# A key selection moved from a block of its own into the loops of two attentions

## The chip, the core and the metric

The kernel is one program on one core of a Trainium2 chip. The metric is the device time of one execution in microseconds (us). TensorE does the matrix products; VectorE, ScalarE and GpSimd work on vectors; SyncE issues the transfers from the chip's memory. The profile calls them PE, DVE, ACT, POOL and SP.

## The reference, cut to what matters

512 tokens of width 1024 go through a first block with four kinds of sequence mixers and a feed-forward part, and then through two layers of a second block. A layer of the second block is a feed-forward part, four mixers side by side, and another feed-forward part. The four mixers have four heads of 64 each: MLA (softmax attention on low-rank queries and keys), NSA (a compressed, a selected and a windowed softmax attention, weighted by gates), DSA (softmax attention on chosen keys) and stick-breaking attention. Their outputs are normalized in groups and multiplied by one output matrix. The part that matters here is DSA, which chooses for each query the 128 keys with the highest index scores:

```
n_top = min(DSA_TOPK, S // 4)                     # 128
rel = relu(einsum('bqhd,bsd->bqhs', qi, k_idx))
score = einsum('bqh,bqhs->bqs', wi, rel)
score = where(k_pos <= q_pos, score, NEG_INF)
_, idx = lax.top_k(score, n_top)
...                                               # softmax attention over the keys idx alone
```

## The kernel before

Queries and keys come in four tiles of 128 tokens. A query tile `i` sees the first `i + 1` key tiles, so the scores of tiles 1, 2 and 3 are 256, 384 and 512 columns wide; tile 0 needs no choice. The large products run as three passes over a high and a low part of each factor; ScalarE writes the high part of the weights and VectorE the low part (lines 447, 448, 454 and 455), and these pieces have high priority.

The code names only the engine of each instruction. A planner sets the order at compile time: it runs through the program in a simulated time, and on each engine takes, of the instructions whose inputs are ready there, the one that stands earliest in the program (or has high priority). On the chip each engine then works through its own list in that fixed order. `_dep` (line 335) adds an order between two instructions to what the planner has to keep; it is declared `NoSync`, so between two instructions of one engine it is their place in the list and nothing else.

`mixers` (line 1250) writes out one layer in this order:

- index queries and keys, then `dsa_score` (line 1451): the index scores of tiles 1 to 3, added up over eight heads on VectorE (line 1480) into `acc`;
- `compress`, then `stick` (line 1632) in turns with the projections of the other mixers, `mla_prep` (line 1383), and the compressed part of `nsa` (line 1569);
- `center` (line 576): the mean over the features is taken off the residual stream;
- the first attention (MLA, `attend` with `mla[0]`, line 1314), in turns with the stacking of NSA's queries and keys and with the product of the stick-breaking output (`out_part(3, ...)`);
- the second attention (NSA, line 1316), in turns with the product of the first one's output;
- `dsa_top` (line 1486): for each of the tiles 1 to 3, 16 rounds. A round finds the eight largest scores of each row (`max`, line 1496) and overwrites them in place (`match_replace`, line 1497; the profile shows a value load and a replacement for it). After 16 rounds the overwritten places are the 128 chosen keys, and line 1498 makes the mask `sel`;
- the third attention (DSA), whose scores take `sel` in through one more product, and the products that are left.

`attend` (line 1354) has eight units: two pairs of heads times four query tiles. A unit of MLA has two softmaxes (`softmax_t`, line 913), one of NSA four. A softmax is: scores on TensorE, the row maximum on VectorE (line 924), the exponential on ScalarE, a guard and the reciprocal on VectorE (lines 931 and 932), scaling on GpSimd (line 934 or 936), transposes on TensorE (line 939), a copy on ScalarE, and the product with the values. `interleave` (line 285) draws one unit from each generator in turn, and so sets the place in the program.

Of the kernel before, what the change touches and what calls it, by code (L numbers as in the profile page):

```python
# [14 lines left out]
ALU = mybir.AluOpType  # L15
# [18 lines left out]
# ---------------------------------------------------------------- host layout  # L34
# [3 lines left out]
def _blocks_t(w):  # L38
    """[K, C] -> chunks of at most RAW columns per partition: [128, blocks of 128 columns, K/128, 128], flat."""
    k, c = w.shape  # L40
    kt = k // 128
    t = w.reshape(kt, 128, c // 128, 128).transpose(1, 2, 0, 3)
    n, per = c // 128, RAW // k
    return np.concatenate([t[:, i:i + per].reshape(-1) for i in range(0, n, per)])


def _blocks_m(w):
    """[K, C] -> per 256 columns: [128, K/128, 256], flat."""
    k, c = w.shape
    return w.reshape(k // 128, 128, c // 256, 256).transpose(2, 1, 0, 3).reshape(-1)  # L50
# [24 lines left out]
def _small(w, axis):  # L75
    """The narrow columns of the first projection on rows 0, 32, 64 and 96 of one block."""
    def z(n):
        s = list(w.shape)
        s[axis] = n
        return np.zeros(s, w.dtype)  # L80

    def c(n):
        sl = [slice(None)] * w.ndim
        sl[axis] = _cols(IN1, n)
        return w[tuple(sl)]

    return np.concatenate([c("mi"), z(28), c("mf"), z(28), c("ga"), z(16), c("ff"), z(28)], axis=axis)


# rows of a head of 64 that is turned: the two of a pair lie 16 apart, as in a head of 32  # L90
# [183 lines left out]
# ---------------------------------------------------------------- device  # L274
def turns(*gens):
    """The units of several generators in turn."""
    gens = list(gens)
    while gens:
        for g in list(gens):
            try:  # L280
                next(g)
            except StopIteration:
                gens.remove(g)
            else:
                yield
# [11 lines left out]

class Builder:
# [17 lines left out]
    # -- small helpers  # L316
# [23 lines left out]
    def table(self, s):  # L340
        """Functions of one table set run together: what follows waits for what came before."""
        if s == self.set:
            return
        b = self.nc.scalar.preload_act_table_set(self.LOADS[s])  # L344
        for g in self.group:
            self._dep(b, g)
        if self.barrier is not None:
            self._dep(b, self.barrier)
        self.set, self.group, self.barrier = s, [], b
# [15 lines left out]
    def add_p(self, out, a, b, op=ALU.add):  # L365
        """out = a op b on GpSimd."""
        self.nc.gpsimd.tensor_tensor(out, a, b, op)
# [13 lines left out]
    def stack_q(self, tag, z, eng):  # L381
        """Two heads of 64 rows, each as its high and low parts one above the other; the high part where the head
        lay."""
        res = []
        for s, e in enumerate(eng):
            q = self.t(tag, dt=F32R)
            a, b = slice(64 * s, 64 * s + 64), slice(64 - 64 * s, 128 - 64 * s)
            self.copy_a(q[a], z[a])
            e.tensor_tensor(q[b], z[a], q[a].bitcast(F32), ALU.subtract)
            res.append(q)  # L390
        return res

    def stack_k(self, tag, z, a, eng):
        """64 rows a of z: their high part twice, their low part twice."""
        hi, lo = self.t(tag, dt=F32R), self.t(tag, dt=F32R)
        for s in range(2):
            self.copy_a(hi[64 * s:64 * s + 64], z[a])
        for s, e in enumerate(eng):
            e.tensor_tensor(lo[64 * s:64 * s + 64], z[a], hi[a].bitcast(F32), ALU.subtract)
        return hi, lo  # L400

    def stacked(self, ps, q, k, h, i):
        """Scores of head h of query tile i, K = 64, at full rate (256 columns at least)."""
        w = max(256, (i + 1) * 128)
        cs, r = slice(i * 128, i * 128 + 128), slice(64 * (h % 2), 64 * (h % 2) + 64)
        self.mm(ps[:, :w], q[h][:, cs], k[0][:, :w], True, False)
        self.mm(ps[:, :w], q[h][r, cs], k[1][r, :w], False, False)

    # -- weights
    def wstream(self, name, nhalf, F, lo_pool=False, center=False, tag=None, alt=()):  # L410
        """Blocks of the weights, F columns each: a list of pieces (hi, lo). center: the mean over all columns is
        taken off each row (for all blocks in one chunk). The pieces lie in tiles of `tag` if it is given; so do the
        blocks in `alt`, in tiles of "PT"."""
# [47 lines left out]
    @staticmethod  # L461
    def cut(pieces, c=128):
        """(hi, lo) of c columns each."""
        return [(hi[:, o:o + c], lo[:, o:o + c]) for hi, lo in pieces for o in range(0, hi.shape[1], c)]
# [9 lines left out]
    def lead(self, jobs, xs):  # L474
        """Up to four blocks (weights, epilogue) side by side, one half of the tokens after the other."""
        ps = [self.p(tag) for tag in ("mm", "mm", "T", "T")[:len(jobs)]]
        for cs in HALVES:
            for k in range(len(xs)):
                for o, (w, _) in zip(ps, jobs):
                    self.passes(o, w, k, xs[k], cs, len(xs))  # L480
        for o, (_, epi) in zip(ps, jobs):
            epi(o)
# [4 lines left out]
    def gemm_blocks(self, name, nblk, xs, epi, lead=0, lo_pool=False, center=False, hold=0, st=None):  # L487
        """out[block of 128 columns, token] for each block; xs: (hi, lo) per 128 rows of the weights.
        The first `lead` blocks run side by side, one half of the tokens after the other. The last `hold` blocks
        follow the attention."""  # L490
# [15 lines left out]
    def gemm_halves(self, name, xs, epi, between, center):  # L506
        """As gemm_t for few rows of weights, all of them on chip: first the one half of the tokens."""
# [14 lines left out]
    def gemm_m_blocks(self, name, ncol, xs, epi, lo_pool=False):  # L522
        """out[token, 256 columns]; epi(chunk, token tile, psum)."""
# [15 lines left out]
    # -- norms  # L539
    def rstd(self, out, in_, scale, eps):  # L540
        """(scale * in + eps) ** -0.5"""
# [3 lines left out]
    def rms_full(self, xs, gain):  # L545
        """rms_norm over all features of the blocks xs; (hi, lo) per block."""
# [23 lines left out]
    def center(self, xs, after=None):  # L570
        """The mean over all features is taken off xs."""
# [16 lines left out]
    class Norm:  # L588
        """x * gain / sqrt(mean(x ** 2) + eps) (+ beta) over blocks of features that are completed one by one,
        first for one half of the tokens. In place or apart."""  # L590
# [7 lines left out]
        def add(self, d, cs):  # L598
            """Squares, added up in pairs."""
# [37 lines left out]
    # -- everything  # L637
# [29 lines left out]
    # ================================================================ first block  # L667
# [147 lines left out]
    def log_sigmoid(self, out, x, tmp):  # L815
        """min(x, 0) - log(1 + exp(-|x|))"""
# [11 lines left out]
    def row(self, r, sign=1):  # L828
        """lhsT that spreads row r over 128 partitions (with all 128 rows as the contraction)."""
# [5 lines left out]
    def keep(self, ap, pattern_sign, base, op):  # L835
        """Zero where not (pattern_sign * (free - partition) + base op 0)."""
# [76 lines left out]
    def softmax_t(self, i, scores, gate=None, add=None):  # L913
        """P^T of query tile i of a causal softmax: [keys, key tile, queries]. scores fills a psum tile;
        add: something to add to the scores."""
# [16 lines left out]
        nc.vector.reciprocal(st[:, 2:3], st[:, 1:2])  # L932
# [208 lines left out]
    # ================================================================ second block  # L1141
    def ffn(self, f, l, xs, hl, norm):
        """alpha x + 0.5 swiglu(x), in place; returns the norm of that."""
# [95 lines left out]
    def rope(self, x, *parts):  # L1239
        """In place. parts: (dimension of the heads, their rows)."""  # L1240
# [9 lines left out]
    def mixers(self, l, hl, xs, norm, last):  # L1250
# [63 lines left out]
        interleave(self.attend(l, mla[0], y, 0), chain([None] * 2, nsa[1]()),  # L1314
                   out_part(3, True, normed(3)))
        interleave(self.attend(l, nsa[0], y, 1), out_part(0, False, normed(0)))
        res1 = normed(1)
        sel = self.dsa_top(accs)
# [35 lines left out]
    def attend(self, l, srcs, y, n, cuts=(slice(0, S),)):  # L1354
        """Four heads of 64. srcs(h, i): list of ("att", scores, gate, value of key tile j) or
        ("mm", lhsT, rhs) for query tile i, whose results add up."""
# [94 lines left out]
    def dsa_score(self, l, iq, misc, tok, accs):  # L1451
        """The products of high and low parts lie one above the other: high, low, high of a query's head on high,
        high, low of the key."""
# [32 lines left out]
    def dsa_top(self, accs):  # L1486
        """Per query tile, 0 for chosen keys and a large negative number for the others."""
        nc = self.nc
        tile = self.t("sel", (128, 1280), BF16)
        sel = [tile[:, 0:128], tile[:, 128:384], tile[:, 384:768], tile[:, 768:1280]]  # L1490
        nc.vector.tensor_copy(sel[0], self.negT)
        for i in range(1, NT):
            acc = accs[i]
            m8 = self.t("m8", (128, 8))
            for r in range(16):
                nc.vector.max(m8, acc)
                nc.vector.match_replace(acc, m8, acc, -3e38)
            nc.vector.tensor_scalar(sel[i], acc, -2e38, NEG, ALU.is_ge, ALU.mult)
        return sel
# [15 lines left out]
    def compress(self, l, cmp):  # L1515
        """Compressed keys (twice, one above the other) and values (four times)."""
# [29 lines left out]
        # gelu(x) = x / (1 + exp(-2 c (x + 0.044715 x^3)))  # L1546
# [22 lines left out]
    def nsa(self, l, comp, nq, nk, tok, res):  # L1569
        nc = self.nc  # L1570
        kc, vc = comp
        # gates
# [124 lines left out]
```

## Time and profile before

| what | value |
|---|---|
| time, median of 3 runs | 3370.67 us (3363.62 to 3381.74) |
| profiled execution, span | 3371.6 us |
| TensorE busy | 3267.3 us (97%) |
| VectorE busy | 1664.1 us (49%) |
| ScalarE busy | 1248.5 us (37%) |
| GpSimd busy | 425.8 us (13%) |
| mean granted clock of TensorE | 0.973 of 2.4 GHz |

The rows further down come from one profiled execution. "Busy" is the time in which an engine works on an instruction; a TensorE that is busy needn't be at its peak. The granted clock is the share of full speed at which TensorE was let run: 1.00 is 2.4 GHz, 0.50 is 1.2 GHz. "Idle before" is an engine's idle time ahead of an instruction, with the one that ended it. Times of day are us from the start of the span. The first layer's mixers lie from about 1410 to 1850 us, the second layer's some 1158 us later.

### The profile page before, as it was taken

The page shows a single profiled execution, that of the slowest core. Times are in us where ns is not written, and L with a number is a line of the kernel's source. Part 1 is how long each engine was busy: PE and PEld are TensorE (multiplying, and loading weights), DVE is VectorE, ACT ScalarE, POOL GpSimd, SP SyncE. Part 2 cuts the span into 40 slices and gives each one's busy share as a digit, 9 for nine tenths or more (in the row PEclk, how much of TensorE's full clock was granted, in tenths as well). Part 3 has the DMA queues.
Part 4 walks back from the last instruction along what each step waited for, and adds up shares of the span by engine and source line. Part 5 has one row for each costly group of instructions (what it writes and reads, how often), then busy time and mean ns, then how long its engine had stood idle before and what let it go on. Part 6 is the DMA issues. An engine that isn't in the chain of part 4 may idle for free.

```text
span 3371.6 us, 41243 instructions
## 1 busy us (share of the span) xinstructions
PE 3267.3 (97%) x16394; PEld 2642.9 (78%) x16398; DVE 1664.1 (49%) x2801; ACT 1248.5 (37%) x2225; POOL 425.8 (13%) x509
## 2 busy tenths in 40 slices
PE   8999999999999999999899999999999998999998
PEld 7798787888888888886567888788888764688887
DVE  4245444454333333579845333553336886453335
ACT  4354624343222222345544322332223445542223
POOL 0001001100000000231523000120004223220002
PEclk9999999999999999999879999999999897899999
DMA  3222222322222222321000222222222310012222
GB/s 134 85 75 79 78 97 85 118 88 100 97 91 100 88 96 92 113 89 53 26 26 26 100 100 89 99 76 100 88 100 76 103 45 31 14 51 100 100 91 72
DMA packets 53071, 275.58 MB, mean 82 GB/s; under 512 B 11136, under 2 KB 16144, under 8 KB 22416
## 3 DMA queue, kind: packets, MB, share of 16 engines
q1 hardware_dynamic: 52736, 272.83, 23.0%
q8 instruction: 129, 2.11, 0.3%
q14 instruction: 62, 0.51, 0.0%
q10 hardware_dynamic: 144, 0.12, 0.0%
HBM read 267.69 MB, written 2.10 MB: 80 GB/s over the span
## 4 chain that ended last, share of the span: by engine, by line
PE 87%; DVE 7%; ACT 3%; issue 1%; POOL 1%; DMA 1%; SPq 0%; ACTq 0%; DVEq 0%; POOLq 0%
PE mm L370 72%; PE S L370 6%; PE T L370 4%; PE O L370 4%; PE T L939 2%; POOL x L630 1%; DVE x L586 1%; DVE wlo L455 1%; DMA wraw<-ffn_w 1%; DVE yc L1245 1%; DVE x L620 0%; ACT L344 0%; ACT whi L363 0%; DVE gt L448 0%; DVE acc L1480 0%
## 5 line engine op out<-in xcount | busy, mean ns | idle before, releaser
L370 PE MATMUL mm<-ahl,whi 128*128 128x512 f32 (+1 forms) x5104 | 1552.1, 384 | 19.2 <-DVE ahl L634 7.6
L370 PEld LDWEIGHTS mm<-ahl,whi 128*128 128x128 f32 x5104 | 944.6, 189 | 216.5 <-issue 11.4
L363 ACT ACTIVATE whi<-wraw 128x1024 fp32r<-128x1024 f32 (+1 forms) x457 | 481.9, 1056 | 1500.7 <-PE mm L370 1406.1
L370 PE MATMUL mm<-ahl,wlo 128*128 128x512 f32 (+1 forms) x2552 | 971.9, 382 | 0.2
L455 DVE TENSOR_TENSOR wlo<-wraw,whi 128x1024 fp32r<-128x1024 f32 (+1 forms) x451 | 573.6, 1273 | 666.3 <-ACT whi L363 658.3
L370 PE MATMUL mm<-hz,whi 128*128 128x512 f32 x1792 | 560.2, 394 | 1.3 <-DVE x L1175 1.3
L370 PEld LDWEIGHTS mm<-ahl,wlo 128*128 128x128 f32 x2552 | 481.8, 189 | 94.8 <-DVE wlo L455 2.8
L370 PEld LDWEIGHTS mm<-hz,whi 128*128 128x128 f32 x1792 | 336.1, 188 | 81.2 <-DVE x L1175 3.0
L370 PE MATMUL mm<-hz,wlo 128*128 128x512 f32 x896 | 352.3, 394 | 0.0
L574 POOL TENSOR_TENSOR ss<-x,x 128x512 f32<-128x512 f32 x6 | 8.7, 1444 | 1564.5 <-DVE x L1175 1564.5
L370 PEld LDWEIGHTS mm<-hz,wlo 128*128 128x128 f32 x896 | 168.2, 188 | 39.8
L370 PE MATMUL mm<-whi,ahl 128*128 128x256 f32 x896 | 170.1, 289 | 7.2 <-DVE hz L1280 6.3
L1157 DVE SCALAR_TENSOR_TENSOR tA<-mm,tA 128x512 f32<-128x512 f32 x80 | 55.2, 690 | 242.3 <-PE mm L370 242.3
L370 PEld LDWEIGHTS mm<-whi,ahl 128*128 128x128 f32 x896 | 143.2, 194 | 11.8 <-DVE hz L1280 6.8
L370 PE MATMUL mm<-wlo,ahl 128*128 128x256 f32 x448 | 128.2, 287 | 1.5 <-DVE wlo L455 1.5
L1175 DVE TENSOR_TENSOR x<-x,mm 128x512 f32<-128x512 f32 x64 | 43.5, 685 | 140.4 <-PE mm L370 140.1
L924 DVE TENSOR_REDUCE sm<-S 128x1 f32<-128x256 f32 (+3 forms) x128 | 61.9, 487 | 97.9 <-PE S L370 91.0
L363 ACT ACTIVATE PT<-T 128x128 f32<-128x128 f32 (+3 forms) x146 | 63.4, 440 | 112.6 <-PE T L939 108.1
L370 PE MATMUL O<-PT,hz 128*64 128x128 f32 (+2 forms) x776 | 92.3, 299 | 2.2 <-ACT PT L363 2.2
L363 ACT ACTIVATE hz<-tA 128x512 fp32r<-128x512 f32 (+1 forms) x124 | 76.0, 617 | 48.3 <-DVE tA L800 40.6
L374 DVE TENSOR_TENSOR hz<-tA,hz 128x512 fp32r<-128x512 f32 (+1 forms) x124 | 82.4, 669 | 20.2 <-ACT hz L363 19.7
L370 PEld LDWEIGHTS mm<-wlo,ahl 128*128 128x128 f32 x448 | 86.9, 194 | 2.6 <-DVE wlo L455 2.1
(350 smaller groups left out, 3687.5 us busy)
## 6 DMA issues: line engine op xcount, KB each, us to landing
wraw<-ffn_w SPq DMA_DIRECT2D x132, 1024.0 KB, 4.8
wraw<-w_gate SPq DMA_DIRECT2D x16, 1024.0 KB, 4.8
wraw<-w_up SPq DMA_DIRECT2D x16, 1024.0 KB, 4.8
wraw<-w_dn SPq DMA_DIRECT2D x16, 1024.0 KB, 4.8
wraw<-w_br SPq DMA_DIRECT2D x8, 1024.0 KB, 4.8
wraw<-w_out SPq DMA_DIRECT2D x8, 1024.0 KB, 4.8
wraw<-w_o SPq DMA_DIRECT2D x4, 768.0 KB, 4.3
gt<-PT SPq DMA_DIRECT2D x48, 64.0 KB, 2.0
```

What stands on the lines that cost most here:

```text
L363: self.nc.scalar.activation(out, in_, AF.Copy)
L370: return self.nc.tensor.matmul(out, lhsT, rhs, start=start, stop=stop, skip_group_check=True)
L374: self.nc.vector.tensor_tensor(lo, src, hi.bitcast(F32), ALU.subtract)
L455: nc.vector.tensor_tensor(lo, r, hi.bitcast(F32), ALU.subtract)
L574: i = nc.gpsimd.tensor_tensor(s1, xs[0], xs[1], ALU.add)
L586: nc.vector.tensor_tensor(xs[d], xs[d], m0, ALU.subtract)
L630: nc.gpsimd.tensor_scalar(y, y, 1.0, be, ALU.mult, ALU.add)
L924: nc.vector.reduce_max(st[:, 0:1], ps, axis=AX.X, negate=True)
L939: nc.tensor.transpose(pt[:, j * 128:j * 128 + 128], P[:, j * 128:j * 128 + 128], self.ident)
L1157: nc.vector.scalar_tensor_tensor(s, ps, 0.5, s, ALU.mult, ALU.mult)
L1175: nc.vector.tensor_tensor(x, x, ps, ALU.add)
L1245: nc.vector.tensor_tensor(xr[r], xr[r], self.c2(f"sin{dim}")[r], ALU.mult)
```

## The change

`dsa_top` becomes a generator that takes the list `sel` to fill and a number `per`. Ahead of each third round it orders the `max` behind the newest softmax reciprocal (`self.soft`, kept in `softmax_t`), and it hands back control after each third round. `slots` draws eight such pieces beside the eight units of the first attention and eight beside those of the second: 16 pieces of three rounds are the 48 rounds of a layer. The rest of the diff removes comments.

```diff
+def slots(gen, n):
+    for _ in range(n):
+        next(gen)
+        yield
...
-        nc.vector.reciprocal(st[:, 2:3], st[:, 1:2])
+        self.soft = nc.vector.reciprocal(st[:, 2:3], st[:, 1:2])
...
-        interleave(self.attend(l, mla[0], y, 0), chain([None] * 2, nsa[1]()),
+        sel = []
+        top = self.dsa_top(accs, sel, 3)
+        interleave(self.attend(l, mla[0], y, 0), slots(top, 8), chain([None] * 2, nsa[1]()),
                    out_part(3, True, normed(3)))
-        interleave(self.attend(l, nsa[0], y, 1), out_part(0, False, normed(0)))
+        interleave(self.attend(l, nsa[0], y, 1), slots(top, 8), out_part(0, False, normed(0)))
         res1 = normed(1)
-        sel = self.dsa_top(accs)
...
-    def dsa_top(self, accs):
+    def dsa_top(self, accs, sel, per):
         nc = self.nc
         tile = self.t("sel", (128, 1280), BF16)
-        sel = [tile[:, 0:128], tile[:, 128:384], tile[:, 384:768], tile[:, 768:1280]]
+        sel += [tile[:, 0:128], tile[:, 128:384], tile[:, 384:768], tile[:, 768:1280]]
+        n = 0
         nc.vector.tensor_copy(sel[0], self.negT)
         for i in range(1, NT):
             acc = accs[i]
             m8 = self.t("m8", (128, 8))
             for r in range(16):
-                nc.vector.max(m8, acc)
+                b = nc.vector.max(m8, acc)
+                if n % per == 0:
+                    self._dep(b, self.soft)
                 nc.vector.match_replace(acc, m8, acc, -3e38)
-            nc.vector.tensor_scalar(sel[i], acc, -2e38, NEG, ALU.is_ge, ALU.mult)
-        return sel
+                if r == 15:
+                    nc.vector.tensor_scalar(sel[i], acc, -2e38, NEG, ALU.is_ge, ALU.mult)
+                n += 1
+                if n % per == 0:
+                    yield
```

## Rows read from the trace of the kernel before

**Rows 1.** The page, part 1: busy time, share of the span, instructions.
```profile
PE 3267.3 (97%) x16394; PEld 2642.9 (78%) x16398; DVE 1664.1 (49%) x2801; ACT 1248.5 (37%) x2225; POOL 425.8 (13%) x509
```

**Rows 2.** Tile acc, 1490 to 1600: min/median/max ns, first and last start, forms.
```profile
L1496 DVE MAX8 m<-acc x48: 406/542/695, 1496.8 to 1588.9; 128x8 f32<-128x256 f32 x16, 128x8 f32<-128x384 f32 x16, 128x8 f32<-128x512 f32 x16
L1497 DVE MATCH_VALUE_LOAD acc<-m,acc x48: 22/80/92, 1498.3 to 1590.9; 128x8 f32 x48
L1497 DVE MATCH_REPLACE8 acc<-m,acc x48: 397/542/676, 1498.3 to 1590.9; 128x256 f32<-128x256 f32 x16, 128x384 f32<-128x384 f32 x16, 128x512 f32<-128x512 f32 x16
L1480 DVE SCALAR_TENSOR_TENSOR acc<-tA,sm,acc x19: 483/603/2632, 1489.9 to 1526.5; 128x384 f32<-128x384 f32 x7, 128x512 f32<-128x512 f32 x7, 128x256 f32<-128x256 f32 x5
```

**Rows 3.** Windows, layer 0: length, busy PE, PEld, DVE, ACT, POOL; PEclk, DMA.
```profile
1520.00:1543.00 23.00, 20.17 (x118) 13.86 (x118) 22.90 (x75) 14.55 (x38) 6.36 (x14) 1.00 0.14 45
1543.00:1602.00 59.00, 59.00 (x287) 42.24 (x286) 51.19 (x110) 25.82 (x49) 7.47 (x14) 1.00 0.16 55
1602.00:1644.00 42.00, 28.12 (x111) 17.70 (x109) 41.50 (x72) 17.15 (x37) 25.36 (x17) 0.81 0.07 26
1644.00:1682.00 38.00, 35.50 (x174) 22.55 (x174) 31.44 (x77) 26.85 (x70) 15.56 (x21) 0.90 0.08 28
1682.00:1728.00 46.00, 46.00 (x164) 26.24 (x164) 15.04 (x54) 17.65 (x52) 10.59 (x16) 0.51 0.07 24
1728.00:1766.00 38.00, 38.00 (x232) 24.26 (x231) 19.45 (x61) 19.12 (x56) 9.41 (x16) 1.00 0.08 29
```

**Rows 4.** Timeline of DVE: start, duration, instruction, idle before and its releaser.
```profile
1590.93 0.67 DVE L1497 MATCH_REPLACE8 acc<-m,acc 128x512 f32<-128x512 f32 x1
...
1598.04 0.75 DVE L448 SCALAR_TENSOR_TENSOR wlo<-wraw,rm,whi 128x512 fp32r<-128x512 f32 x1 [2.45 <-ACT whi L447]
```

**Rows 5.** Windows, layer 1, the columns as in rows 3.
```profile
2672.00:2690.00 18.00, 15.94 (x70) 12.52 (x68) 15.06 (x45) 7.01 (x21) 4.41 (x7) 0.62 0.23 66
...
2760.00:2802.00 42.00, 26.92 (x113) 17.27 (x111) 41.48 (x72) 17.12 (x37) 25.34 (x17) 0.84 0.07 25
2802.00:2842.00 40.00, 38.71 (x178) 23.71 (x178) 28.51 (x73) 26.59 (x67) 14.55 (x20) 0.83 0.08 27
...
2888.00:2924.00 36.00, 36.00 (x223) 23.03 (x223) 17.97 (x58) 18.68 (x55) 8.96 (x15) 1.00 0.09 30
```

**Rows 6.** The chain that ended last, 1470 to 1860: shares of it by line.
```profile
by line: PE mm L370 31.6%; PE S L370 17.8%; PE O L370 11.7%; PE T L939 6.3%; PE T L370 6.2%; DVE acc L1480 2.5%; issue 2.5%; DVE yc L1245 1.7%; DVE x L586 1.6%; DVE acc L1497 1.5%; DVE m L1496 1.4%; POOL x L630 1.1%; DVE gt L1432 0.8%; DVE 
```

**Rows 7.** Windows of line 1496 alone, then of line 1497 alone: DVE busy.
```profile
1496.00:1592.00 96.00, 25.45 (x48) 1.00 0.24 80
1496.00:1592.00 96.00, 28.33 (x96) 1.00 0.24 80
```

**Rows 8.** Timeline of PE, 1522 us.
```profile
1522.05 1.06 PE L370 MATMUL mm<-gt,gt 128*68 128x128 f32 x8 [2.06 <-POOL wlo L367]
```

**Rows 9.** Waits, 1644 to 1803: us in total, times, longest us.
```profile
POOL tA L936 <- DVE sm L932: 39.5, 15, 7.8
```

**Rows 10.** Lines of DVE, 1644 to 1682: busy us, mean ns, idle before.
```profile
L448 DVE SCALAR_TENSOR_TENSOR gt<-wraw,rm,gt 128x256 fp32r<-128x256 f32 x4 | 2.4, 615 | 0.0
L427 DVE TENSOR_REDUCE rm<-wraw 128x1 f32<-128x1024 f32 x2 | 2.3, 1211 | 0.0
```

**Rows 11.** Timelines of DVE and PE at the end of the second attention.
```profile
1765.19 0.15 DVE L932 RECIPROCAL sm<-sm 128x1 f32<-128x1 f32 x1
...
1777.43 0.39 PE L370 MATMUL S<-sel,identb 128*128 128x512 bf16 x1
```

**Rows 12.** Windows of 6 us around two falls of the clock.
```profile
1632.00:1638.00 6.00, 1.83 (x6) 0.85 (x5) 5.94 (x8) 0.81 (x4) 5.29 (x4) 0.50 0.00 0
1680.00:1686.00 6.00, 6.00 (x28) 4.20 (x29) 4.05 (x17) 4.57 (x15) 2.87 (x4) 0.50 0.00 0
1674.00:1680.00 6.00, 4.33 (x22) 2.42 (x20) 5.93 (x14) 5.95 (x15) 2.91 (x3) 0.90 0.01 3
```

## What I predict

> **What bounds the kernel now.** I read the page's busy shares first, then windows over the second block's two layers, then the chain of waits there, then the rounds' own rows. TensorE is busy 97% of the span and VectorE 49% [rows 1]; that share of VectorE is an average, so the stage decides. One round is a MAX8, a value load and a replacement. There are 48 per layer, and before the change VectorE runs all of them from 1497 to 1591 us (layer 1: some 1158 us later), during the stick-breaking attention and the projections, although the code places them after the second attention [rows 2]. The layer-0 stretches [rows 3] show what that costs:
> - 1520 to 1543: VectorE is full (22.90 of 23 us), TensorE loses 2.83 us.
> - 1543 to 1602: VectorE 51.19 of 59 us, TensorE loses nothing.
> - 1602 to 1644: VectorE is full (41.50 of 42) and TensorE idles 13.9 us. No round is in here: the last one starts at 1590.93, and VectorE then sat idle 2.45 us for ScalarE's weights [rows 4], so it had no backlog left from them.
> - 1644 to 1682, most of the first attention (MLA): VectorE 31.44 of 38 us, TensorE 35.50.
> - 1682 to 1728, the first half of the second attention (NSA): VectorE 15.04 of 46 us, TensorE full but at a granted clock of 0.51.
> - 1728 to 1766, its second half: VectorE 19.45 of 38, TensorE full at full clock.
> Layer 1 has the same picture [rows 5]. In the chain from 1470 to 1860 the rounds hold 1.5% and 1.4% of 390 us, some 11 us [rows 6], but TensorE works beside nearly all of it.
>
> **The price of the rounds.** By the windows of the two lines alone, VectorE is busy 25.45 + 28.33 = 53.8 us with them per layer [rows 7]. There are 16 rounds each of 256, 384 and 512 columns, and the min, median and max of MAX8 are 406, 542 and 695 ns [rows 2]; the replacements stand nearly the same, so I share the 53.8 us out as 0.25, 0.33 and 0.42: 13.3, 17.8 and 22.7 us. The change does not alter what a round costs: while GpSimd worked in the same stretch, the two-input line L1480 once took 2632 ns, but no MAX8 exceeded 695 [rows 2]. The lower bound of this price is no change from 53.8; the upper is the unoverlapped sum, 16 x (0.41+0.54+0.70) x 2 + 48 x 0.08 = 56.6 us. I take 53.8, since other VectorE work stands between the rounds after the change too.
>
> **What is removed: the rounds beside the projections.** The gain is TensorE's loss there, not VectorE's 53.8 us. Layer 0: 2.83 us from 1520 to 1543, of which 2.06 is one wait that the profile puts on GpSimd's weight split [rows 8]. Layer 1: 2.06 us from 2672 to 2690, where the granted clock is also 0.62, worth up to 0.38 x 15.94 = 6 us [rows 5]. Bounds for both layers together: 0 and 11 us. I take 6, the middle, since the rounds share the queue with the copies that TensorE then waits for but aren't the releaser named. The idle from 1602 to 1644 stays: its queue holds no round.
>
> **What is added: 24 rounds beside each attention.** `slots` issues three rounds after each of the eight units of an attention. The first of three is tied to the latest reciprocal, and the other two follow through the scores that they rewrite. Both instructions are VectorE's, so the tie is an order in its queue, with no semaphore. Behind the rounds in that queue stand the maxima and reciprocals of the next softmaxes; GpSimd's scaling already waits most for these reciprocals (39.5 us in 15 waits) [rows 9], and TensorE's transposes wait for the scaling. No DMA is moved, and nothing goes past SP's or GpSimd's queue.
> - First attention: 16 rounds of 256 and 8 of 384 columns, 13.3 + 8.9 = 22.2 us. VectorE has 38 - 31.44 = 6.6 us free in layer 0 and 40 - 28.51 = 11.5 us in layer 1 [rows 3, 5]. The overflow is 15.6 + 10.7 = 26 us. Bounds: 16, if the reductions and splits of the next product's weights (2.3 + 2.4 us of the 31.44, not due yet [rows 10]) slip into the second attention in both layers; and 34, if VectorE packs to 93% only, a share between the 87% of 1543 to 1602 and the 99% of 1602 to 1644 (53.6/0.93 - 38 and 50.7/0.93 - 40). I take 26, no slip and no gaps, as the stretch before it ran at 99%. TensorE's work cannot cover this: its own 35.5 us lie beside the first 38, and the next attention's softmaxes need VectorE as well.
> - Second attention, first half: 8 of 384 and 4 of 512, 8.9 + 5.7 = 14.6 us into 31 free: nothing. The cover is TensorE at half clock; without it (23 us shorter) only 8 us would be free and 7 would show.
> - Second half: 12 of 512, 17.0 us into 18.6 free (18.0 in layer 1). That is filled to 96%, and in-order waiting must cost something: 0 to 6 us per layer, and I take 3, so 6.
> - The last key tile's mask: the last reciprocal of the second attention is at 1765.19, three rounds and the mask end near 1770, and TensorE first reads it at 1777.43 [rows 11]. Hidden with 7 us to spare.
>
> **The sum.** -6 + 26 + 0 + 6 = +26 us on the profiled execution's span of 3371.6 us, which is 0.9 us from the median (3370.67): 3397 us, 0.8% slower. From the bounds: 3371 - 11 + 16 + 0 = 3376 to 3371 + 34 + 12 = 3417. About 0.5% (17 us) is what a measurement of this kernel can tell from no change.
>
> **Rivals.**
> *Hidden anyway* (3371). The first attention's overflow is 26 us only if the VectorE work of 1644 to 1682 stays there. Both attentions together have VectorE 66 us busy of 122 in layer 0; 66 + 54 = 120 still fits. If the planner spreads the surplus into the half-clock stretch, the overflow drops to the gain's size. For it: the 31 us free there. Against: the rounds come ahead of later softmaxes in program order, and the tie keeps them beside their own.
> *The projections unclog* (3343, faster). The planner lays the whole queue out anew. If the rounds' 11 us on the chain do hold up what ends in 1602 to 1644, TensorE wins back its idle time there too: 2.8 + 13.9 in layer 0, 2.1 + 6 + 15.1 in layer 1, some 40 us, against about 12 us lost in the attentions: -28, 3343. It decides from the point where VectorE reaches the rope and compression work before 1602 instead of after. For it: VectorE is 100% busy there and heads the chain. Against: TensorE was full until 1602, so the inputs of that work come no sooner.
> *The clock falls* (3420). When TensorE idled from 1632 to 1638 (1.83 us busy of 6) the granted clock went to 0.50 (1.2 GHz); from 1680 it was at 0.50 with TensorE fully busy, after 1.67 us idle in the 6 us ahead [rows 12]. TensorE's work from 1644 to 1682 is 35.50 x 0.90 = 32 us at full clock, so 64 at half; against the 54 that VectorE needs that is 10 us more in layer 0, and by the same count (38.71 x 0.83, 51) 13 in layer 1: 3397 + 23. The Trainium skill (TensorE: Matmul & The Clock Gate, Part 1: The HAM clock gate) says that "the default state is throttled, and activity releases the throttle"; by that rule a first attention in which TensorE idles a third of the time tends to this rival, and the trace agrees for 1632.
> *The change does nothing*: excluded, since each round needs the scores of the one before and the first is tied.
>
> **How the numbers follow.** Forecast 0.40 (own range 3384 to 3417), hidden 0.25 (3356 to 3385), unclogged 0.22, clock 0.13. The range reaches from 3340 to 3440, since the new order of the queue moves each case by some 20 us either way: it leaves out the unclogged times below 3340 (0.1) and the clock case's above 3440 (0.05). Faster by over 0.5% (below 3354): 0.22 and a little of hidden, 0.23. Slower (above 3387.5): the forecast's larger part and the clock case, 0.48. The rest, 0.29, is the same within 0.5%.
>
> **What would show it.** Right: no round before the first softmax of the first attention; VectorE nearly full from about 1640 until the first attention ends, which takes 50 us or more in place of 38; TensorE idle there with VectorE's maxima or reciprocals as releasers; the stretch before 1602 hardly shorter. Wrong: the first attention no longer than before, or TensorE's idle time before 1644 shrunk by over 8 us per layer, which would give the second rival. A granted clock of 0.5 through the first attention would give the third.

## The result: slower by 0.7%, and where it went

The changed kernel's median is 3385.5 us in 12 executions, against 3360.4 us for 35 of the kernel before on the same chip: 1.0068, with a 95% interval of 1.0045 to 1.0091. An earlier set of 7 executions each gave 1.0062 (1.0045 to 1.0079). The forecast was +26 us, and some +21 to +25 came, but not out of the stage that the forecast named. The profiled execution of the changed kernel has a span of 3381.8 us. Line numbers of the kernel after are 7 to 13 higher than those of the rows of before in the lines used here (924 became 931, 932 became 939, 939 became 946, 370 became 377, 1496 became 1506, 1497 became 1509, 1498 became 1511).

The windows of the kernel after, layer 0 and then two stages of layer 1, to be read beside [rows 3, 5]: length, busy PE, PEld, DVE, ACT, POOL, then the granted clock, DMA share and GB/s.

```profile
1520.00:1543.00 23.00, 22.21 (x92) 16.27 (x92) 6.80 (x23) 12.73 (x34) 5.30 (x10) 0.78 0.11 34
...
1543.00:1602.00 59.00, 59.00 (x290) 40.31 (x288) 22.48 (x36) 29.06 (x58) 9.95 (x17) 1.00 0.15 54
1602.00:1644.00 42.00, 29.07 (x127) 18.63 (x125) 40.88 (x73) 17.20 (x38) 25.90 (x17) 0.84 0.07 26
1644.00:1687.00 43.00, 39.06 (x202) 24.60 (x202) 41.97 (x131) 30.32 (x77) 15.57 (x21) 0.92 0.08 25
1687.00:1728.00 41.00, 40.34 (x152) 23.30 (x152) 27.03 (x92) 15.17 (x45) 9.72 (x15) 0.58 0.08 27
1728.00:1765.00 37.00, 36.42 (x235) 23.51 (x234) 32.14 (x105) 19.85 (x56) 11.31 (x18) 1.00 0.08 29
1765.00:1808.00 43.00, 36.38 (x213) 23.31 (x212) 28.32 (x82) 22.27 (x63) 7.45 (x16) 1.00 0.00 1
...
2796.00:2842.00 46.00, 41.13 (x198) 26.17 (x198) 45.14 (x131) 29.29 (x74) 16.28 (x21) 0.83 0.07 24
...
2923.00:2972.00 49.00, 42.11 (x208) 25.89 (x208) 28.52 (x81) 22.32 (x62) 7.25 (x16) 0.83 0.00 1
```

The first attention is now 1644 to 1687 and 2796 to 2842, VectorE is full in it, and TensorE idles 3.9 and 4.9 us there. The stage that the prediction left out is the third attention, from the last reciprocal of the second to its own last one: 1765 to 1808 and 2923 to 2972. The same stage of the kernel before, from its own trace:

```profile
1767.00:1808.00 41.00, 38.39 (x227) 25.36 (x226) 21.73 (x65) 22.71 (x64) 9.49 (x17) 0.96 0.00 1
2926.00:2966.00 40.00, 37.24 (x231) 24.75 (x233) 21.61 (x63) 22.71 (x64) 9.41 (x17) 1.00 0.00 1
```

VectorE works 6.6 and 6.9 us longer there than before, and TensorE idles 6.6 us in layer 0 (43 - 36.38) and 6.9 in layer 1 where it idled 2.6 and 2.8. The extra VectorE work is the tail of the rounds. First the 48 MAX8 of each layer as the view of the tile `acc` groups them (minimum, median and maximum ns, first and last start, forms). Then, from VectorE's timeline of layer 0 (start, duration), the last reciprocal of the second attention, the last round's MAX8 and the last mask, and from TensorE's its first product on that mask:

```profile
L1506 DVE MAX8 m<-acc x48: 408/552/695, 1648.3 to 1776.5; 128x8 f32<-128x256 f32 x16, 128x8 f32<-128x384 f32 x16, 128x8 f32<-128x512 f32 x16
...
L1506 DVE MAX8 m<-acc x48: 408/552/696, 2800.0 to 2935.4; 128x8 f32<-128x256 f32 x16, 128x8 f32<-128x384 f32 x16, 128x8 f32<-128x512 f32 x16
```
```profile
1764.16 0.15 DVE L939 RECIPROCAL sm<-sm 128x1 f32<-128x1 f32 x1
...
1776.47 0.69 DVE L1506 MAX8 m<-acc 128x8 f32<-128x512 f32 x1
...
1777.98 0.43 DVE L1511 TENSOR_SCALAR sel<-acc 128x512 bf16<-128x512 f32 x1
```
```profile
1778.46 0.59 PE L377 MATMUL S<-sel,identb 128*128 128x512 bf16 x2
1781.33 0.73 PE L377 MATMUL mm<-ahl,whi 128*128 128x512 f32 x2 [2.27 <-ACT ahl L370]
```

The mask comes 13.8 us after that reciprocal, not the 5 that [rows 11] were read to mean, and the product on it starts 0.05 us after the mask ends. In layer 1 the mask is later still (2939.98, 18.0 us behind the last reciprocal at 2921.96), and the list of TensorE has the product on it behind products of the next stage, so VectorE waits for those scores (VectorE's timeline, then TensorE's; in brackets the idle time before and what ended it):

```profile
2939.98 0.43 DVE L1511 TENSOR_SCALAR sel<-acc 128x512 bf16<-128x512 f32 x1
...
2944.98 1.49 DVE L931 TENSOR_REDUCE sm<-S 128x1 f32<-128x512 f32 x3 [3.97 <-PE S L377]
```
```profile
2944.22 0.95 PE L377 MATMUL S<-sel,identb 128*128 128x512 bf16 x2
```

The stages of all profiled executions, from the timelines of VectorE (layer 0 / layer 1, us). "First" runs from the end of `center` (line 593) to the last reciprocal of the first attention, "second" to that of the second, "third and tail" to the last norm before the feed-forward part (line 627).

| kernel | median us (95% interval of the ratio to the kernel before on the same chip) | first | second | third and tail |
|---|---|---|---|---|
| before | 3364.7 | 38.5 / 43.5 | 85.5 / 81.1 | 75.9 / 74.4 |
| before, second profile | 3359.9 (0.997 to 1.003) | 42.6 / 40.5 | 68.4 / 72.5 | 75.6 / 74.3 |
| after | 3385.9 (1.0045 to 1.0079) | 42.7 / 45.4 | 77.6 / 80.9 | 80.7 / 87.1 |
| after, second profile | 3385.5 (1.0045 to 1.0091) | 42.7 / 45.4 | 76.1 / 68.6 | 83.2 / 84.2 |
| mask of tile 3 first | 3371.2 (1.0018 to 1.0058) | 42.7 / 45.4 | 79.4 / 81.2 | 76.1 / 77.1 |
| four to a piece | 3376.8 (1.0035 to 1.0087) | 40.8 / 42.4 | 80.3 / 81.1 | 83.5 / 90.0 |
| tile 3 beside first attention | 3361.1 (0.998 to 1.002) | 42.4 / 41.8 | 64.8 / 78.3 | 75.8 / 77.2 |
| tile 3 beside second attention | 3360.3 (0.997 to 1.001) | 40.5 / 40.5 | 74.3 / 81.5 | 76.3 / 75.0 |
| all beside second attention | 3404.6 (1.010 to 1.015) | 38.4 / 40.1 | 85.2 / 67.3 | 101.8 / 97.6 |
| no rounds at all | 3353.7 (0.997 to 1.001) | 38.7 / 40.1 | 76.8 / 79.7 | 75.8 / 74.4 |
| 40 rounds | 3356.2 (0.996 to 1.001) | 42.7 / 46.2 | 76.1 / 65.8 | 75.9 / 74.3 |
| tiles 1 and 2 tied | 3358.4 (0.998 to 1.003) | 43.7 / 43.8 | 78.7 / 64.1 | 76.9 / 75.7 |
| two chains | 3389.3 (1.005 to 1.011) | 43.9 / 44.2 | 70.9 / 76.9 | 82.8 / 83.9 |
| no tie | 3365.3 (0.998 to 1.004) | 42.5 / 43.6 | 68.4 / 81.1 | 74.4 / 74.4 |

The second attention varies as much for one kernel (68.4 to 85.5 us before) as between kernels; it follows the granted clock. So a pair of profiles does not show the whole loss: the spans of the two pairs of before and after differ by 10.2 and 13.3 us, the medians by 21 and 25. The last column repeats within 1 us for the kernel before, and it sorts the kernels: 149 to 153 us for both layers together where no mask is late, 167 to 199 in the five profiles of the four kernels with late masks.

### The profile page after: what moved, and what is told of

Read it like the earlier page. It is cut to its first block, busy times and chain, and to the rows that moved or that the text cites. A ratio compares the mean times of both kernels' runs of the same rounds, so it can differ in the third digit from the quotient of the medians.

```text
span 3381.8 us, 41261 instructions
## 1 busy us (share of the span) xinstructions
PE 3269.0 (97%) x16398; PEld 2641.1 (78%) x16398; DVE 1650.4 (49%) x2801; ACT 1252.0 (37%) x2225; POOL 425.5 (13%) x509
## 4 chain that ended last, share of the span: by engine, by line
PE 87%; DVE 7%; ACT 2%; DMA 1%; POOL 1%; issue 1%; SPq 0%; ACTq 0%; POOLq 0%; DVEq 0%
PE mm L377 72%; PE S L377 6%; PE T L377 4%; PE O L377 3%; PE T L946 1%; POOL x L637 1%; DVE wlo L462 1%; DVE x L593 1%; DMA wraw<-ffn_w 1%; DVE yc L1252 1%; DVE x L627 0%; ACT whi L370 0%; DVE sm L931 0%; DVE rm L434 0%; DVE gt L455 0%
## 5 line engine op out<-in xcount | busy, mean ns | idle before, releaser
L377 PEld LDWEIGHTS mm<-ahl,whi 128*128 128x128 f32 x5104 | 945.6, 189 | 222.4 <-ACT ahl L370 13.8
L377 PEld LDWEIGHTS mm<-hz,whi 128*128 128x128 f32 x1792 | 336.3, 188 | 81.1 <-DVE x L1182 3.0
L1182 DVE TENSOR_TENSOR x<-x,mm 128x512 f32<-128x512 f32 x64 | 43.5, 685 | 140.4 <-PE mm L377 140.1
L377 PEld LDWEIGHTS O<-PT,hz 128*64 128x64 f32 (+2 forms) x776 | 60.1, 151 | 33.7 <-issue 17.1
```

Of the source, the lines that this page charges most:

```text
L377: return self.nc.tensor.matmul(out, lhsT, rhs, start=start, stop=stop, skip_group_check=True)
L1182: nc.vector.tensor_tensor(x, x, ps, ALU.add)
```

## The experiments

**Theory A**: the loss is the last mask, which comes too late for the third attention. **Theory B**, the prediction's: VectorE's surplus of work lengthens the first attention. All edits are to the changed kernel.

**Both kernels once more.** 

> The kernel before, once more, for a second profile beside one of the changed kernel: the median of seven runs was 3364.7 us, so 3360 to 3372. Both theories want the same of it: first attention 38 to 44 us long, third attention without a stall at the mask of tile 3. If its stages move by several us from the first profile, only differences larger than that can be read from single profiles.

> The changed kernel, once more: 3383 to 3390 us, 1.005 to 1.008 of the kernel before. Theory A (the last mask is late): the third attention is longer than before by 2 to 10 us per layer, with TensorE's product on the mask starting only after the mask, while the first attention gains no more than 6 us per layer. Theory B (the first attention is too full, as predicted): the first attention is longer by 10 us or more per layer in this profile, and the third by little.

Measured: 3359.9 and 3385.5 us. The first attention lasts 42.7 and 45.4 us in both profiles of after; of the kernel before it lasts 38.5 to 43.5 us, 41.3 on average, so the change adds 2.7 us per layer. The third attention with its tail is 17.5 us longer than before, both layers together, in the first pair of profiles and in the second. The profiles speak for A.

**The mask of tile 3 ahead of its rounds.**

```diff
             for r in range(16):
+                if i == 3 and r == 0:
+                    nc.vector.tensor_scalar(sel[i], acc, -2e38, NEG, ALU.is_ge, ALU.mult)
...
-                if r == 15:
+                if r == 15 and i < 3:
```

> The mask of tile 3 is made ahead of its 16 rounds instead of behind them, so the computation leaves out the choice for tile 3; all 48 rounds still run in their places. Theory A: the third attention no longer waits for the last round, and 10 to 17 us of the loss come back: 3369 to 3376 us. Theory B: VectorE's load beside the first two attentions is unchanged, so 3382 to 3390 us. A rival to both, that the new order of the whole queue costs the time wherever it falls: also 3380 or more, with the loss in other stages.

Measured: 3371.2 us, 14.4 less than the changed kernel, with every round still in place. The third attention with its tail is back at 76.1 and 77.1 us, 14.2 less in both layers than in the second profile of after. That is A's. It is still 0.38% slower than the kernel before.

**Four rounds to a piece.**

```diff
-        top = self.dsa_top(accs, sel, 3)
+        top = self.dsa_top(accs, sel, 4)
...
-        interleave(self.attend(l, nsa[0], y, 1), slots(top, 8), ...
+        interleave(self.attend(l, nsa[0], y, 1), slots(top, 4), ...
```

> Four rounds to a piece instead of three: 32 rounds beside the first attention (all of tiles 1 and 2), 16 beside the first half of the second, none beside its second half. Theory A: the mask of tile 3 is ready some 20 us before it is read, so the third attention stands as before, 10 to 17 us less than the changed kernel, against up to 5 us more in the first attention: 3370 to 3380 us. Theory B: the first attention carries 8 rounds of 384 columns more, 8.9 us per layer that find no room: 3395 to 3405 us.

Measured: 3376.8 us. The time is in A's range, but not for A's reason: the rounds end no earlier than in the changed kernel, and the last mask starts 17.6 and 24.7 us behind the second attention's last reciprocal. The MAX8 and the masks of tiles 2 and 3 in layer 0:

```profile
L1506 DVE MAX8 m<-acc x48: 400/551/694, 1645.1 to 1777.0; 128x8 f32<-128x256 f32 x16, 128x8 f32<-128x384 f32 x16, 128x8 f32<-128x512 f32 x16
```
```profile
L1511 DVE TENSOR_SCALAR sel<-acc x2: 350/386/422, 1751.0 to 1779.5; 128x384 bf16<-128x384 f32 x1, 128x512 bf16<-128x512 f32 x1
```

So the mask was late again and the median doesn't tell A from B. The lower median is the clock's: at a mean granted clock of 0.977 to 0.979 this kernel took 3372.7 to 3377.8 us (7 executions) and the changed one 3368.0 to 3372.8 (3), at 0.971 to 0.973 it took 3389.0 to 3393.8 (5) against 3382.9 to 3392.0 (8). The run also tells that the pieces' size doesn't set the end: 15 rounds lie within the first attention of layer 0, where the program has 32, and the changed kernel has 15 to 16 of 24.

**Tile 3 alone, beside the first attention.**

```diff
-                if n % per == 0:
+                if i == 3 and n % per == 0:
                     self._dep(b, self.soft)
...
-                if n % per == 0:
+                if i == 3 and n % per == 0:
                     yield
```

(`per` is 2, with eight pieces beside the first attention and none beside the second.)

> The rounds of tiles 1 and 2 are untied and free to run early, as before; the 16 rounds of tile 3 are tied in pairs beside the first attention: 22.7 us of rounds there, as in the changed kernel (22.2), but with the last mask done long before it is read. Theory A (the late mask and what follows from it): the third attention stands as before, and the time is 3358 to 3368 us. Theory B (VectorE too full beside the first attention): the first attention loses what the changed kernel loses there, 3375 to 3388 us.

Measured: 3361.1 us, the kernel before's time. Ten of the 16 rounds lie within the first attention in each layer; their MAX8 take 6.84 us there in layer 0, where the changed kernel's 15 take 6.49 (the same view of both: line 1506's busy time in the first attention; the first line is this run's):

```profile
1646.90:1689.30 42.40, 6.84 (x10) 0.87 0.07 26
```
```profile
1644.10:1686.70 42.60, 6.49 (x15) 0.92 0.08 26
```

The same VectorE work beside the first attention as in the changed kernel, and no loss: this work is not what the changed kernel loses by, and B falls as the cause. What the 22 us that the prediction put there would cost stays unmeasured, since in no run did more than 16 rounds lie within the first attention.

**Tile 3 alone, beside the second attention** (`per` is 4, four pieces).

> As the run before it, but the 16 rounds of tile 3 are tied in fours beside the first half of the second attention, where VectorE was least busy. Both theories want no loss: 3355 to 3365 us, or below that by what 45 us less VectorE work in two layers beside the projections is worth, 0 to 5 us. A third explanation, that any tie that reorders the queue costs some 20 us, wants 3375 or more.

Measured: 3360.3 us. Sixteen rounds tied to the first four units still run from 1695.0 to 1760.2 us. So a new order of the queue costs nothing by itself, and there is no gain that can be told from zero.

**All rounds beside the second attention** (`per` is 6, eight pieces there and none beside the first).

> No rounds beside the first attention; six rounds tied to each of the eight units of the second. Theory A: 54 us of rounds in a chain cannot end with the second attention, so the mask is later than in the changed kernel (by 10 us or more) and the third attention waits longer: 3395 to 3415 us. Theory B: the first attention is as before, and the second, 31 + 19 us free, is overfull by about 4 us per layer: 3365 to 3375 us.

Measured: 3404.6 us, +43. The first attention is as before, and the mask comes at 1805.6 us, 42 us behind the second attention. Now TensorE is seen waiting for it, in the list of waits of the third attention (layer 0; total us, times, longest):

```profile
PE S L377 <- DVE sel L1511: 10.2, 1, 10.2
```

No loss where the mask is done before the last reciprocal of the second attention, +25 us where it comes 14 and 18 us behind it, +43 at 42. A stands; B would have had no loss of its own in the first attention, and a small one here.

**No rounds.**

> All 48 rounds of each layer are left out, so the keys are not chosen; the masks are made of the scores as they are. It gives the most that any place for the rounds can bring. If the rounds cost the kernel before only TensorE's losses at 1520 to 1543 and 2672 to 2690, as the prediction took it, 3349 to 3360 us, 0 to 11 less than before. If they also hold up the work that TensorE waits for from 1602 to 1644 (the second rival), 3320 to 3335 us.

Measured: 3353.7 us, 7.6 less than the kernel before, with an interval that takes in no change (0.9966 to 1.0005). The second rival falls with it, as TensorE's idle time of 1602 to 1645 is there without any round:

```profile
1602.00:1645.00 43.00, 29.44 (x128) 18.81 (x127) 41.43 (x75) 17.43 (x38) 25.91 (x17) 0.83 0.07 25
```

**Forty rounds, eight of them for tile 3.**

```diff
-            for r in range(16):
+            for r in range(16 if i < 3 else 8):
```

(The mask of tile 3 follows its eighth round, and 14 pieces take the 40 rounds.)

> As the changed kernel, but tile 3 gets 8 rounds instead of 16, so it chooses only 64 keys; all else stands in its place. At the measured pace of 2.7 us per round the last mask is done some 20 us earlier, before the third attention reads it. Theory A (the late mask is the loss): 3360 to 3366 us, as the kernel before. If what was left when the mask was made first (some 10 us over the kernel before) comes from the first attention's 16 rounds or from the queue's new order, it stays: 3368 to 3374 us.

Measured: 3356.2 us. Its rounds and softmaxes stand as in the changed kernel up to the end, its first attention is as long (42.7 and 46.2 us), and its last round starts at 1754.3 us, before the second attention's end:

```profile
L1506 DVE MAX8 m<-acc x40: 407/546/690, 1645.3 to 1754.3; 128x8 f32<-128x256 f32 x16, 128x8 f32<-128x384 f32 x16, 128x8 f32<-128x512 f32 x8
```

Eight late rounds per layer, 2 x 11.3 us of VectorE work, decide over 29 us of the median.

**Tiles 1 and 2 tied, tile 3 early.**

```diff
-        for i in range(1, NT):
+        for i in (3, 1, 2):
...
-                if n % per == 0:
+                if i < 3 and (n - 16) % per == 0:
                     self._dep(b, self.soft)
```

(The 32 tied rounds take 11 pieces, eight beside the first attention and three beside the second.)

> The 16 rounds of tile 3 are untied and run early; the 32 of tiles 1 and 2 are tied three at a time beside the first attention and the first units of the second. The first attention carries what it carries in the changed kernel (16 rounds within its span), and every mask is done before it is read. Theory A: 3358 to 3364 us. If the first attention's rounds cost something of their own: its 2 us more in layer 0 and 3 in layer 1 show, 3364 to 3370 us. Theory B in its predicted size (26 us): 3380 us or more.

Measured: 3358.4 us. The first attention lasts 43.7 and 43.8 us with 15 rounds in it per layer. Its 2 to 3 us more are there and do not show in the time.

**Two chains**: each piece has one round of tile 3 and two of tile 1 or 2.

> The same 48 rounds in the same 16 pieces of three, but each piece has one round of tile 3 and two of tile 1 or 2, so two chains run side by side. If the rounds lag their softmaxes because each waits for the one before it, the two chains end earlier and the third attention waits less: 3365 to 3375 us. If they lag because VectorE's queue as a whole is behind, the last rounds end as late as before and two masks are late instead of one: 3383 to 3392 us.

Measured: 3389.3 us. The rounds end where they did, 1774.9 us, though none of tile 3's 16 has to wait for those of tiles 1 and 2 any more:

```profile
L1505 DVE MAX8 m<-acc x48: 408/554/690, 1648.4 to 1774.9; 128x8 f32<-128x512 f32 x16, 128x8 f32<-128x256 f32 x16, 128x8 f32<-128x384 f32 x16
```

So a round's wait for the one before it does not set the pace; VectorE's list as a whole is behind.

**No tie**: the two lines with `_dep` are left out.

> The rounds stay where the change puts them in the program, but without the order behind a softmax's reciprocal. If the tie is what moves them, they run early beside the projections, and the time is the kernel before's: 3355 to 3368 us. If their place in the program alone is enough, 3380 us or more.

Measured: 3365.3 us, the same as before. The tie alone moves the rounds, not their place in the program:

```profile
L1506 DVE MAX8 m<-acc x48: 412/546/695, 1497.8 to 1594.6; 128x8 f32<-128x256 f32 x16, 128x8 f32<-128x384 f32 x16, 128x8 f32<-128x512 f32 x16
```

**All runs at the same clock.** Over the 108 executions of the kernel before, the time follows the mean granted clock along a straight line: 2.7 us more for each 0.001 less, with a scatter (standard deviation) of 1.3 us. Against that line, each execution at its own clock, the medians are +9.5 us for the changed kernel, +13 for four to a piece, +21 for two chains and +29 for all rounds beside the second attention; they are +2 with the mask first, -1 with forty rounds, +2 with tiles 1 and 2 tied, +5 and +4 with tile 3 alone, -2.5 without rounds and 0 without the tie. So at the same clock, too, the kernels with late masks lose most, and of the two where only the last mask is late, the one with the later mask loses more (14 and 18 us: +9.5; 18 and 25: +13). The rest of the 25 us goes with the lower clock.

No version that computes the whole result is told from the kernel before as faster: what a perfect place for the rounds could bring is at most the 7.6 us of the run without them, which are not told from zero.

## Why the prediction came out right in its sum and wrong in its terms

- **The rounds' price** (53.8 us per layer): right. From 1640 to 1780 the MAX8 and the replacements take 26.0 us each, 55.0 with the value loads by the windows of [rows 7], and a MAX8 is as long as before (408, 552, 695 ns). The costliest lines of VectorE in that window (busy us, mean ns, then the idle time before them and what ended it):

```profile
L1509 DVE MATCH_REPLACE8 acc<-m,acc 128x256 f32<-128x256 f32 (+2 forms) x48 | 26.0, 544 | 0.0
L1506 DVE MAX8 m<-acc 128x8 f32<-128x256 f32 (+2 forms) x48 | 26.0, 552 | 0.0
L931 DVE TENSOR_REDUCE sm<-S 128x1 f32<-128x256 f32 (+3 forms) x52 | 25.2, 485 | 16.9 <-PE S L377 14.3 <-POOL tA L943 2.5
```

- **What is removed** (-6, bounds 0 and -11): within its bounds, and no sharper than that. In layer 0 TensorE wins back 2.04 us from 1520 to 1543 (22.21 busy against 20.17), though that window's clock is 0.78 there instead of 1.00. The run without rounds puts the whole gain at 7.6 us, with an interval that takes in none.
- **The idle time of 1602 to 1644 stays**: right. TensorE idles 12.9 us (13.9 before), VectorE 40.88 of 42 us busy with no round in front of it.
- **First attention** (+26, whose lower bound of 16 should read 17, 26.3 less twice 4.7): this term is mis-sized; about +5 came (2 x 2.7). The step that failed is "24 rounds beside each attention". VectorE is full, as forecast, but only 15 of the 24 rounds lie in layer 0's first attention, 6.49 us of MAX8 and 7.44 of value loads and replacements, 13.9 us in place of 22.2. The tie sets the earliest place of a piece and nothing its latest, so the rest slid into the second attention. This was the first rival's mechanism (it "spreads the surplus into the half-clock stretch").
- **Second attention** (+6): within its bounds of 0 and 12 or below; it lasts 68.6 to 80.9 us after and 68.4 to 85.5 before, so a few us can't be told. But the first half did not take the surplus in. From 1686.7 to 1728 there were 14 rounds, where the program has 12 and 8 or 9 were owed, with VectorE 27 of 41 us busy. I argue, and did not show, that in-order waiting sets this: in this list the rounds stand behind maxima that wait for TensorE's scores (line 931 above, 14.3 us). In VectorE's timeline:

```profile
1720.85 0.54 DVE L1509 MATCH_REPLACE8 acc<-m,acc 128x384 f32<-128x384 f32 x1
...
1724.19 0.29 DVE L931 TENSOR_REDUCE sm<-S 128x1 f32<-128x128 f32 x1 [2.72 <-PE S L377]
...
1725.24 0.55 DVE L1506 MAX8 m<-acc 128x8 f32<-128x384 f32 x1
```

- **The last mask** ("hidden with 7 us to spare", 0): wrong, and this is where the loss is. The reciprocal at 1765.19 was the last but one: GpSimd's last scaling of the second attention starts at 1767.09, behind the reciprocal of 1766.74, so by the prediction's own count the spare was 6 us. The step that failed reckons three rounds behind the last reciprocal. That held only if the first 45 were done by then; in layer 0 five rounds start behind it, beside the third attention's own maxima. The third attention with its tail grew by 17.5 us, and making the mask earlier gave 14.4 us back.
- **The clock** (third rival): wrong in its place, since the first attention has 0.92 and 0.83, about as before [rows 3, 5], but the clock has the larger share of the loss. The mean granted clock has a median of 0.972 over the 12 executions after, and 0.978 over 108 of the kernel before. At the same mean, 0.972, the spans are 3384.9 (5 executions) and 3376.7 us (5): 8 us apart. The other two thirds of the loss come with more time at 1.2 GHz. One part of it stands in the third attention with its tail: of the 17.5 us there, 7.5 in the first pair of profiles and 8.5 in the second are idle time of TensorE, and the other 9.9 and 9.1 are busy time, for about as many products at a lower clock. Layer 1 of that stage, before and then after:

```profile
2925.60:3000.10 74.50, 69.73 (x472) 54.36 (x470) 47.77 (x116) 43.02 (x113) 25.45 (x40) 1.00 0.09 29
```
```profile
2922.10:3009.20 87.10, 78.52 (x466) 58.34 (x464) 55.09 (x137) 44.05 (x111) 24.98 (x40) 0.88 0.07 25
```

The lower clock stands around the new idle times, in the profile of after:

```profile
2938.00:2946.00 8.00, 7.14 (x26) 4.54 (x26) 4.03 (x9) 2.18 (x5) 0.00 (x0) 0.57 0.00 0
2960.00:2976.00 16.00, 12.53 (x43) 6.75 (x44) 5.03 (x17) 6.97 (x18) 2.54 (x4) 0.57 0.00 1
```

  Ahead of the first, TensorE idles 2.79 us for the second attention's normed output. A clock of 0.57 over 24 us is up to 10 us of work; the kernel before has 1.00 throughout that stage in layer 1.

The forecast's sign was right for another reason than its own, and its size by luck, because two errors met: 21 us too many in the first attention, 17.5 missing in the third. The signs that the prediction asked for came half true: VectorE full, no round before the first softmax, no shorter stretch before 1602; but the first attention is no 50 us long, and its waits are not for VectorE's maxima.

**What stays open.** With the mask made first, the time is still 10 us over the kernel before, and 3 of them stand in the third stage. The run of forty rounds, alike but for the eight rounds left out, has none of the 10. The mean granted clock has medians of 0.9745 and 0.9795 in the two, so most of the rest comes with the clock (at the same clock 2 us are left); why eight rounds at the start of the third attention go with it was not settled, nor why one execution has half clock in the second attention where another has full, nor where the part of the lower clock falls that the third stage doesn't show. Nor was it settled which entries of VectorE's list set the pace of about 2.7 us per round (130 us for 48).

## What to carry to other kernels

A tie that says "not before this softmax" gives no due time: before you count a moved chain as hidden, follow its end to the first reader at the pace that the queue really allows (here 2.7 us per round beside softmaxes against 2.0 beside the projections), not at the pace of the loop that issues it. Work that is free of the critical path may fill any gap early, but each step that it is put off uses up slack that someone downstream needs; the largest gain on offer here was 7.6 us, not told from zero, and the chain's late end came with 25, of which 9.5 stay at the same clock. Where a forecast is a sum of terms, check each term's stage in the trace afterwards, since a right total can hide two wrong ones; and compare medians at the same granted clock, since a kernel that looked 9 us better here (four to a piece) was the slower one.

## What was not expected of the hardware

One program's executions differ by 40 us (3342.9 to 3382.6 in 45 of the kernel before) and the difference follows the mean granted clock: it is 0.984 at spans of 3341 to 3344 us and 0.971 at 3378 to 3380. Between the two profiles of the kernel before most of it lies in the second attention, where one profile of the kernel before has 0.51 for 46 us [rows 3] and the other has, from 1691 to 1728 us, with TensorE as busy:

```profile
1691.00:1728.00 37.00, 37.00 (x209) 23.33 (x209) 18.44 (x65) 20.23 (x61) 12.40 (x20) 0.92 0.08 29
```

The Trainium skill (TensorE: Matmul & The Clock Gate, Part 1: The HAM clock gate) says that activity releases the throttle; the trace agrees only in part, for the kernel after has 0.58 from 1687 to 1728 us with TensorE busy for 40.34 of 41 us. A single profile of this kernel therefore can't carry a difference of 10 us in that stage, while the stage behind it repeats within 1 us in the kernel before (within 3 us in the kernel after).
